# Experts: a new layout of the gates in DRAM, an earlier place for a load in the code, and other buffers for the last residuals

## The chip, the cores and the metric

One core of one Trainium2 chip runs the whole kernel. The metric is device time in microseconds (us); the kernel before took 4202.12 us (median of 3 runs, 4198.15 to 4209.2). A core has five engines that run beside each other: TensorE (PE; its weight loads are PEld), VectorE (DVE), ScalarE (ACT), GpSimd (POOL) and SyncE (SP). SP here only issues DMAs. All DMAs of the core share 16 DMA engines; those that SP issues go through one hardware queue (q1), the indirect gathers that POOL issues through another (q0).

## The reference, cut to what matters

The block is a trunk layer over 1024 tokens of width 1024 (two mixing branches, then a retrieval over experts). The change lies in the retrieval and in the end of the block:

```python
def peer(h, wq, subkeys, u_tab, v_tab):
    ...
        s1, i1 = lax.top_k(s[:, :, 0], PEER_TOPK)
        s2, i2 = lax.top_k(s[:, :, 1], PEER_TOPK)
        ...
        idx = e1 * PEER_KEYS + e2
        gate = jax.nn.softmax(sc, axis=-1).astype(hb.dtype)
        act = jax.nn.gelu(jnp.einsum('td,thkd->thk', hb, u_sel), approximate=False) * gate
        return jnp.einsum('thk,thkd->td', act, v_sel)
...
        h_lat = h_lat + g2_l * peer(f_l, ...)
    return rmsnorm(h_lat, final_norm)
```

Each token picks 128 of 16384 experts (8 heads of 16). An expert is a row of `u_tab` and a row of `v_tab`, 1024 numbers each. The result is multiplied by a gain row `g2_l`, added to the stream `h_lat`, and normalised.

## The kernel before, in words

The 1024 tokens are treated in two ways. Five blocks of 128 tokens (640 tokens, `TD`) are computed densely: the experts form 128 tiles of 128 experts, every tile's scores are computed for all 640 tokens and multiplied by a gate that is zero where a token did not pick the expert. The other three blocks (384 tokens) are computed by gathering: for each of the 128 picks POOL issues one indirect DMA of 128 rows of `u` (or `v`), 768 gathers of 512 KB in all, and DVE multiplies each gathered buffer (`rows`, 7 buffers) into a running sum `e_p`.

**Gates.** In a first stage `spread` makes the dense gates. For each 32 tokens it fills a tile `r_st` of 128 partitions (expert within its tile) by 128 tiles by 32 tokens, and SP writes it to DRAM as one of the 20 slices of `G` (line 1471). A partition's piece is 16 KB in one run, on both sides.

**The expert loop** (`run`) goes over 32 groups of four tiles. For a group, `gates` (line 1614) loads `x_g`: for each of 128 partitions 20 pieces (one per 32 tokens) of four tiles by 32 tokens, which is 512 bytes each. `up` makes the scores of one tile: PE multiplies `x_raw` (loaded by SP, split in a high and a low part on ACT and on DVE or POOL) with the tokens into `x_s` (line 1634), ACT applies the gelu into `x_a`, DVE multiplies with `x_g` (line 1651), ACT and DVE split the product (`x_ah`, `x_al`). For 48 of the tiles (`AHEAD`) the scores were computed during the first stage, written to DRAM as `A`, and `up` loads them instead (line 1647). `down` multiplies the group's products with the `v` rows into PSUM `x_acc` (line 1674), and DVE adds that to the sum `x_o` (line 1680). The `v` rows come in halves of 512 columns: SP loads `x_vr` (2 buffers, 256 KB each, line 1602), ACT and POOL split it into `x_vh` and `x_vl` (lines 1605, 1606). The next load of `x_vr` waits until POOL has made the `x_vl` of the one two before it.

**The end.** `finish` closes a gathered block: it loads the block of `h`, the gain row `g` and the final norm's row `fin` into `rows` buffers, forms g times sum plus h, and `norm` squares it on ACT into the buffer of `h`, scales it on DVE and writes it out. `last_half` does the same for the five dense blocks: it loads the gain and the norm row once more, loads five blocks of `h` into `rows` buffers, lets POOL do the residual of the first 512 columns (lines 1569, 1570) and DVE that of the second half.

**Order.** The code is recorded in program order, and a scheduler with a simulated clock sets the order of instructions on each engine. Each engine and SP's queue then run strictly in that order: an instruction that waits holds up all behind it on its engine.

Of the kernel before, what the change touches and what calls it, by code (L numbers as in the profile page):

```python
# [10 lines left out]
F32 = mybir.dt.float32  # L11
# [10 lines left out]
D = 1024  # L22
# [1182 lines left out]
def colrows(t, n, c0=0, w=D):  # L1205

    return bass.AP(tensor=t.tensor, offset=t.offset + 8 * n * D + c0, ap=[[D, 8], [64 * D, 16], [1, w]])
# [69 lines left out]
ND = 5  # L1277
TD = ND * 128
NG = NB - ND
NT = 128  # L1280
GT = 32
SC = 4
# [8 lines left out]
class Route:  # L1291
# [94 lines left out]
    def second(self, b, wk):  # L1386
# [25 lines left out]
        nc.scalar.activation(pof, pos, AF.Copy)  # L1412
        up = wk.tile([128, 8, 16], F32, name="r_up", bufs=1)
        V.tensor_scalar(up, pof[:, 0], 4.0, None, op0=ALU.is_ge)
        V.scalar_tensor_tensor(pof[:, 2], pof[:, 2], 12.0, pof[:, 0], op0=ALU.subtract, op1=ALU.subtract)
        V.tensor_sub(pof[:, 3], pof[:, 3], pof[:, 1])
# [24 lines left out]
    def spread(self, b, ef, g, wk, ps, pq):  # L1441

        K, nc = self.K, self.K.nc
        V = nc.vector
        p = ps.tile([128, 4, 128], F32, name="qt", bufs=1)
        for j, x in enumerate((ef[:, 1], ef[:, 0], g)):
            nc.tensor.transpose(p[:, j], x, K.ident)
        T = wk.tile([128, 3, 128], F32, name="r_T", bufs=2)
        nc.scalar.activation(T, p[:, :3], AF.Copy)
        for q in range(128 // GT):  # L1450
            st = wk.tile([128, 128, GT], F32, name="r_st", bufs=2)
            for t8 in range(GT // 8):
                t0 = q * GT + t8 * 8
                ts = slice(t0, t0 + 8)
                io = self.iota[:, None, :].to_broadcast([128, 8, 128])
                e0 = wk.tile([128, 8, 128], F32, name="r_e0", bufs=2)
                V.tensor_tensor(e0, io, T[:, 0, ts, None].to_broadcast([128, 8, 128]), op=ALU.is_equal)  # L1457
                e2 = wk.tile([128, 8, 128], F32, name="r_e2", bufs=3)
                V.tensor_tensor(e2, io, T[:, 1, ts, None].to_broadcast([128, 8, 128]), op=ALU.is_equal)  # L1459
                e1 = wk.tile([128, 8, 128], F32, name="r_e1", bufs=2)  # L1460
                nc.gpsimd.tensor_mul(e1[:, :GP], e0[:, :GP], T[:, 2, t0:t0 + GP, None].to_broadcast([128, GP, 128]))
                for m in range(GP, 8):
                    nc.scalar.activation(e1[:, m], e0[:, m], AF.Copy, scale=T[:, 2, t0 + m:t0 + m + 1])
                for t4 in range(2):
                    pg = pq.tile([128, 4, 128], F32, name="qg", bufs=3)
                    for m in range(4):
                        nc.tensor.matmul(pg[:, m], e1[:, t4 * 4 + m], e2[:, t4 * 4 + m], start=True, stop=True)
                    o = t8 * 8 + t4 * 4
                    nc.scalar.activation(st[:, :, o:o + 4], pg.rearrange("p t e -> p e t"), AF.Copy)
                yield  # L1470
            nc.sync.dma_start(K.T["G"][b * (128 // GT) + q], st)


class Experts:
# [77 lines left out]
    def finish(self, b, acc):  # L1552

        V = self.K.nc.vector
        h, g, fin = self.row(), self.row(), self.row()
        self.K.nc.sync.dma_start(h, self.K.T["h1"][b * 128:(b + 1) * 128, :])
        self.ends(g, fin)
        V.tensor_mul(g, g, acc)
        V.tensor_add(g, g, h)
        self.norm(b, g, h, fin)  # L1560

    def ends(self, g, fin):

# [7 lines left out]

    def norm(self, b, acc, h, fin):
        K, nc = self.K, self.K.nc
        ss = self.gp.tile([128, 1], F32, name="f_ss", bufs=2)
        nc.scalar.activation(h, acc, AF.Square, accum_out=ss)
        r = K.rstd(self.gp, ss, D, [128, 1], "f_n")
        nc.vector.scalar_tensor_tensor(acc, acc, r[:], fin, op0=ALU.mult, op1=ALU.mult)
        nc.sync.dma_start(colrows(K.o["out"], b), acc)
# [30 lines left out]
    def gates(self, e):  # L1609

        K, nc, wk = self.K, self.K.nc, self.wk
        n = TD // GT
        t = wk.tile([128, n, SC, GT], F32, name="x_g", bufs=GB)
        nc.sync.dma_start(t, K.T["G"].rearrange("q p e t -> p q e t")[:, :, e:e + SC, :])
        return t

    def score(self):
# [20 lines left out]
    def up(self, g, m):  # L1638

        K, nc, wk = self.K, self.K.nc, self.wk  # L1640
        e = SC * g + m
        if m == 0:
            self.g4 = self.gates(e)
            self.A[g] = []
        if e in AHEAD:
            a = wk.tile([128, TD], F32, name="x_a", bufs=XA)
            nc.sync.dma_start(a, K.T["A"][AHEAD.index(e)])
        else:
            a = self.score()
        av = a.rearrange("p (q t) -> p q t", t=GT)  # L1650
        (nc.gpsimd if self.turn('m', MP) else nc.vector).tensor_mul(av, av, self.g4[:, :, m, :])
        hi = wk.tile([128, TD], F32R, name="x_ah", bufs=AB)
        lo = wk.tile([128, TD], F32R, name="x_al", bufs=AB)
        K.split(a, hi, lo)
        self.A[g].append((hi, lo))

    def ahead_v(self, n):

        while len(self.V) < n and self.nv < 2 * NT:
            g, r = divmod(self.nv, 2 * SC)  # L1660
            half, m = divmod(r, SC)
            self.V[g, half, m] = self.load_v(SC * g + m, half)
            self.nv += 1
# [18 lines left out]
    def last_half(self):  # L1682

        g = NT // SC - 1
        gate, fin = self.row(), self.row()
        self.ends(gate, fin)
        for half in range(2):
            hs = slice(half * 512, (half + 1) * 512)
            for b in range(ND):
                if half == 0:  # L1690
                    if b == 0:
                        self.h = []
                    self.h.append(self.row())
                    self.K.nc.sync.dma_start(self.h[b], self.K.T["h1"][b * 128:(b + 1) * 128, :])
                else:
                    self.down(g, 1, b)
                self.residual(self.K.nc.vector if half else self.K.nc.gpsimd, self.acc[:, b, hs], self.h[b][:, hs], gate[:, hs])
                if half:
                    self.norm(b, self.acc[:, b], self.h[b], fin)

    def pour(self, rb):

# [7 lines left out]
    def run(self, pool, wk, ps):  # L1710
        self.wk, self.ps = wk, ps
        self.acc = pool.tile([128, ND, D], F32, name="x_o")
        left = 256 * NG - int(self.done)
        n = NT // SC

        share = (left - LASTG) / (2 * ND * (n - 1) + ND + 2.6 * (NT - NE))
        self.A, self.V, self.nv = {}, {}, 0
        self.ahead_v(SC)
        for m in range(SC):
            self.up(0, m)  # L1720
            self.some(2.6 * share if m not in AHEAD else 0)
        for g in range(n):
            units = [(h, b) for h in range(2 if g < n - 1 else 1) for b in range(ND)]
            for u, (h, b) in enumerate(units):
                if g < n - 1 and u in UPS:
                    e = SC * (g + 1) + UPS.index(u)
                    self.up(g + 1, UPS.index(u))
                    if e not in AHEAD:
                        self.some(2.6 * share)
                self.down(g, h, b)  # L1730
                self.some(share)
            if g:
                self.A.pop(g - 1, None)
        for _ in self.rows:
            pass
        self.last_half()


# [46 lines left out]
XA = 2  # L1785
# [7 lines left out]
AHEAD = [4 * g + m for g in range(32) for m in range(2 - g % 2)]  # L1793
U_ORDER = AHEAD + [e for e in range(128) if e not in AHEAD]
EF = 1
GB = 2
# [3 lines left out]
def back(K):  # L1800
    T, dr = K.T, K.dram
    T["h1"] = dr.tile([L, D], F32, name="d_h1")
    T["f"] = dr.tile([L, D], F32, name="d_f")
    T["G"] = dr.tile([TD // GT, 128, 128, GT], F32, name="d_G")
    T["A"] = dr.tile([max(NE, 1), 128, TD], F32, name="d_A")
    with K.pool("keep") as keep, K.pool("xg") as gp, K.pool("ft", right=True) as ft, K.pool("xu", right=True) as xu:
        R = Route(K, keep)
        R.fTd = [ft.tile([128, 8, TD], F32R, name="fT" + n) for n in "hl"]
        X = Experts(K, R, gp, xu)
        with ExitStack() as late:  # L1810
            with K.pool("rm", right=True) as mid:
                R.tables(mid)
                out_proj(K, R)
                X.gps = late.enter_context(K.pool("xgp", space=PSUM))
                peer(K, X, R)
            X.pour(RB2)
# [107 lines left out]
```

## Time and profile before

| | |
|---|---|
| median of 3 runs | 4202.12 us |
| profiled execution, its own time | 4209.43 us |
| its span in the trace | 4207.5 us |
| PE busy | 3807.4 us (90%) |
| DVE busy | 3385.1 us (80%) |
| POOL busy | 2045.4 us (49%) |
| granted clock of PE, mean | 0.954 |

The durations come from one execution of 4209.43 us, which is 7.3 us above the median. Its span lies 1.9 us below its own time. The expert loop begins at about 2560 us of the span and ends at about 4166 us, with the last matmul.

### The profile page before, as it was taken

How to read it: one execution, taken by the hardware profiler on the slowest of the kernel's cores; microseconds unless marked ns; L12 is line 12 of the kernel's file. 1: busy time of each engine (PE TensorE's matmuls, PEld its weight loads, DVE VectorE, ACT ScalarE, POOL GpSimd, SP SyncE). 2: the span in 40 equal slices, each digit the busy share in tenths (PEclk: the TensorE clock that was granted, in tenths of full speed). 3: DMA queues.
4: the chain of work that ended last, by engine and by line, in shares of the span. 5: the costliest groups of instructions: out<-in, count | busy, mean ns of one | idle time of the engine just before them, and what ended most of it. 6: DMA issues, size and time to landing. Idle time of an engine off the chain costs nothing.

```text
span 4207.5 us, 60407 instructions
## 1 busy us (share of the span) xinstructions
PE 3807.4 (90%) x21993; PEld 3346.8 (80%) x21993; DVE 3385.1 (80%) x5997; ACT 1389.8 (33%) x2674; POOL 2045.4 (49%) x1643
## 2 busy tenths in 40 slices
PE   5999999898898997789999968899989999999996
PEld 3787887787888896689999867788878888788785
DVE  5665787546799795599999996788878889888798
ACT  3233333325563121242236664222222222222221
POOL 2232323344343121066435445666667776777675
PEclk8999999998899998899999999999999999999998
DMA  6333333466766446567546547899989999999897
GB/s 204 110 124 98 125 120 127 133 204 206 235 210 204 152 145 177 175 236 267 197 158 231 191 161 259 284 321 318 348 300 337 326 327 346 337 322 338 317 330 259
DMA packets 509673, 974.12 MB, mean 232 GB/s; under 512 B 33771, under 2 KB 291231, under 8 KB 506432
## 3 DMA queue, kind: packets, MB, share of 16 engines
q1 hardware_dynamic: 395616, 557.25, 40.4%
q0 software_dynamic: 110880, 405.98, 26.3%
q10 hardware_dynamic: 2880, 7.03, 0.5%
q8 instruction: 173, 2.83, 0.3%
q14 instruction: 124, 1.02, 0.1%
HBM read 823.20 MB, written 146.95 MB: 231 GB/s over the span
## 4 chain that ended last, share of the span: by engine, by line
PE 39%; DVE 22%; DMA 13%; issue 7%; POOL 6%; ACT 3%; SPq 1%; POOLq 0%; DVEq 0%; ACTq 0%
PE x_acc L1674 9%; PE x_s L1634 8%; PE mm L199 7%; DMA x_vr<-in_peer_v_dram 6%; POOL rows L1511 3%; DVE rows L1535 3%; PE pe L1134 2%; PE hy L850 2%; POOL x_vl L1606 2%; DVE r_e L1459 2%; PE tp L850 1%; DVE r_e L1457 1%; PE hx L850 1%; DMA s_e<-d_cum 1%; DMA rows<-in_peer_u_dram,ids 1%
## 5 line engine op out<-in xcount | busy, mean ns | idle before, releaser
L1634 PE MATMUL x_s<-fTh,x_uh 128*128 128x320 f32 x2048 | 642.9, 314 | 15.0 <-ACT x_a L1635 15.0
L1634 PE MATMUL x_s<-fTh,x_ul 128*128 128x320 f32 x2048 | 640.1, 313 | 5.5 <-DVE x_ul L1595 5.5
L1634 PE MATMUL x_s<-fTl,x_uh 128*128 128x320 f32 x2048 | 640.5, 313 | 0.0
L1674 PE MATMUL x_acc<-x_vl,x_ah 128*128 128x512 f32 x1280 | 517.2, 405 | 18.3 <-POOL x_vl L1606 18.3
L1674 PE MATMUL x_acc<-x_vh,x_ah 128*128 128x512 f32 x1280 | 451.9, 405 | 85.0 <-ACT x_vh L1605 61.4
L1548 DVE SCALAR_TENSOR_TENSOR e_p<-rows,e_a,e_p 128x1024 f32<-128x1024 f32 x381 | 489.6, 1285 | 35.1 <-DMA rows<-in_peer_v_dram,ids 27.6
L1674 PE MATMUL x_acc<-x_vh,x_al 128*128 128x512 f32 x1280 | 512.2, 402 | 0.0
L1511 POOL DMA_INDIRECT rows<-in_peer_u_dram,ids x384 | 417.7, 1088 | 177.7 <-DVE rows L1535 54.5
L1535 DVE SCALAR_TENSOR_TENSOR rows<-rows,e_p 128x1024 f32<-128x1024 f32 x384 | 456.2, 1210 | 34.1 <-DMA rows<-in_peer_u_dram,ids 33.7
L1511 POOL DMA_INDIRECT rows<-in_peer_v_dram,ids x384 | 402.8, 1049 | 133.1 <-issue 62.9
L1606 POOL TENSOR_TENSOR x_vl<-x_vr,x_vh 128x512 fp32r<-128x512 f32 x256 | 340.1, 1332 | 191.0 <-ACT x_vh L1605 187.6
L1634 PEld LDWEIGHTS x_s<-fTh,x_uh 128*128 128x128 f32 x2048 | 390.5, 191 | 30.1 <-ACT x_a L1635 19.9
L1634 PEld LDWEIGHTS x_s<-fTh,x_ul 128*128 128x128 f32 x2048 | 389.7, 190 | 15.5 <-DVE x_ul L1595 6.9
L1634 PEld LDWEIGHTS x_s<-fTl,x_uh 128*128 128x128 f32 x2048 | 390.4, 191 | 9.4
L1674 PEld LDWEIGHTS x_acc<-x_vh,x_ah 128*128 128x128 f32 x1280 | 242.1, 194 | 139.3 <-ACT x_vh L1605 69.3
L1674 PEld LDWEIGHTS x_acc<-x_vl,x_ah 128*128 128x128 f32 x1280 | 249.8, 195 | 72.0 <-POOL x_vl L1606 26.2
L1605 ACT ACTIVATE x_vh<-x_vr 128x512 fp32r<-128x512 f32 x256 | 160.0, 627 | 423.3 <-DMA x_vr<-in_peer_v_dram 349.6
L1674 PEld LDWEIGHTS x_acc<-x_vh,x_al 128*128 128x128 f32 x1280 | 249.0, 195 | 49.4
L1595 POOL TENSOR_TENSOR x_ul<-x_raw,x_uh 128x1024 fp32r<-128x1024 f32 x57 | 140.3, 2461 | 281.6 <-ACT x_uh L1594 281.3
L199 PE MATMUL mm<-xh,whi 128*128 128x512 f32 (+1 forms) x784 | 263.9, 412 | 7.4 <-DVE acc L235 3.6
L199 PE MATMUL mm<-xl,whi 128*128 128x512 f32 (+1 forms) x784 | 263.8, 411 | 7.1 <-DVE xl L51 7.1
L1594 ACT ACTIVATE x_uh<-x_raw 128x1024 fp32r<-128x1024 f32 x128 | 135.2, 1057 | 400.1 <-PE x_s L1634 355.4
(382 smaller groups left out, 8704.3 us busy)
## 6 DMA issues: line engine op xcount, KB each, us to landing
x_raw<-in_peer_uT_dram SPq DMA_DIRECT2D x128, 512.0 KB
x_vr<-in_peer_v_dram SPq DMA_DIRECT2D x256, 256.0 KB
d_G<-r_st SPq DMA_DIRECT2D x20, 2048.0 KB
x_g<-d_G SPq DMA_DIRECT2D x32, 1280.0 KB
wraw<-in_w_mod_dram SPq DMA_DIRECT2D x32, 1024.0 KB
wraw<-in_w_in_dram SPq DMA_DIRECT2D x24, 1024.0 KB
wk_w<-d_WK SPq DMA_DIRECT2D x24, 1024.0 KB
d_kr<-h_k SPq DMA_DIRECT2D x32, 512.0 KB
```

What stands on the lines that cost most here:

```text
L199: nc.tensor.matmul(p, w[:, k], x[j][:, k, t0:t0 + n], start=(k == 0 and q == 0), stop=(k == 7 and q == 2))
L850: nc.tensor.matmul(out, self.m[mats][:, tl, :], x, start=(n == 0), stop=(n == len(terms) - 1))
L1134: nc.tensor.matmul(p, a[:, k], w[:, ss], start=(k == 0 and q == 0), stop=(k == n - 1 and q == 2))
L1511: nc.gpsimd.indirect_dma_start(out=r, out_offset=None, in_=table, in_offset=bass.IndirectOffsetOnAxis(ap=ids[:, j:j + 1], axis=0))
L1535: nc.vector.scalar_tensor_tensor(r, r, 1.0, f, op0=ALU.mult, op1=ALU.mult, accum_out=d[:, j:j + 1])
L1548: nc.vector.scalar_tensor_tensor(acc, r, a[:, j:j + 1], acc, op0=ALU.mult, op1=ALU.add)
L1594: nc.scalar.activation(hi, raw, AF.Copy)
L1595: self.pace = (nc.vector if self.turn('u', UR if self.n < NE else UP) else nc.gpsimd).tensor_sub(lo, raw, hi.bitcast(F32)).ins
L1605: nc.scalar.activation(hi, raw, AF.Copy)
L1606: self.pace = nc.gpsimd.tensor_sub(lo, raw, hi.bitcast(F32)).ins
L1634: nc.tensor.matmul(s[:, :SW], w[:, k], x[:, k, ms], start=(k == 0 and q == 0), stop=(k == 7 and q == 2))
L1674: self.K.nc.tensor.matmul(p, a[x][:, bs], v[w], start=(m == 0 and q == 0), stop=(m == SC - 1 and q == 2))
```

## The change

There are three parts. (a) `G` in DRAM gets the order group, partition, 32-token slice, tile and token. The write of a slice then puts 32 pieces of 512 bytes per partition in 32 places, and a group's load reads one run of 10240 bytes per partition. (b) The load of an `AHEAD` tile stands in the code at the end of the step before. (c) At the end, the blocks of `h` of the dense part go to the two `x_g` buffers (two blocks in each, and one in a `rows` buffer), the last `finish`'s gain and norm rows are kept and used by `last_half`, and `finish` works in the PSUM sum: it multiplies the sum in place, adds it to `h`, and squares into the sum.

```diff
-            nc.sync.dma_start(K.T["G"][b * (128 // GT) + q], st)
+            nc.sync.dma_start(K.T["G"][:, :, b * (128 // GT) + q].rearrange("g p e t -> p g e t"),
+                              st.rearrange("p (g e) t -> p g e t", e=SC))
...
-        V.tensor_mul(g, g, acc)
-        V.tensor_add(g, g, h)
-        self.norm(b, g, h, fin)
+        V.tensor_mul(acc, acc, g)
+        V.tensor_add(h, h, acc)
+        self.norm(b, h, acc, fin)
+        self.gains = g, fin
...
-        nc.sync.dma_start(t, K.T["G"].rearrange("q p e t -> p q e t")[:, :, e:e + SC, :])
+        nc.sync.dma_start(t, K.T["G"][e // SC])
...
         if e in AHEAD:
-            a = wk.tile([128, TD], F32, name="x_a", bufs=XA)
-            nc.sync.dma_start(a, K.T["A"][AHEAD.index(e)])
+            a = self.pre.pop(e) if e in self.pre else self.load_a(e)
...
+        if e + 1 in AHEAD:
+            self.pre[e + 1] = self.load_a(e + 1)
...
-        gate, fin = self.row(), self.row()
-        self.ends(gate, fin)
...
+        gate, fin = self.gains
+        halves = [slice(half * 512, (half + 1) * 512) for half in range(2)]
+        for b in range(ND):
+            self.residual(self.K.nc.gpsimd, self.acc[:, b, halves[0]], self.h[b][:, halves[0]], gate[:, halves[0]])
+        for b in range(ND):
+            self.down(g, 1, b)
+            self.residual(self.K.nc.vector, self.acc[:, b, halves[1]], self.h[b][:, halves[1]], gate[:, halves[1]])
+            self.norm(b, self.acc[:, b], self.h[b], fin)
+
+    def load_h(self):
+
+        self.h = []
+        for b in range(ND):
+            if b == ND - 1:
+                h = self.row()
+            elif b % 2:
+                h = t[:, D:2 * D]
+            else:
+                t = self.wk.tile([128, TD // GT, SC, GT], F32, name="x_g", bufs=GB).rearrange("p q e t -> p (q e t)")
+                h = t[:, :D]
+            self.K.nc.sync.dma_start(h, self.K.T["h1"][b * 128:(b + 1) * 128, :])
+            self.h.append(h)
...
-    T["G"] = dr.tile([TD // GT, 128, 128, GT], F32, name="d_G")
+    T["G"] = dr.tile([NT // SC, 128, TD // GT, SC, GT], F32, name="d_G")
```

On SP's queue in the expert loop, here some groups after its start, the kernel before has these rows (`x_raw` the tiles of `u`, `x_vr` the halves of `v`, `x_a<-d_A` the scores made ahead, `x_g` the gates):

```order
L1602 DMA x_vr<-in_peer_v_dram 128x512 x2
L1647 DMA x_a<-d_A 128x640
L1602 DMA x_vr<-in_peer_v_dram 128x512 x2
L1584 DMA x_raw<-in_peer_uT_dram 128x1024
L1614 DMA x_g<-d_G 128x20x128
L1647 DMA x_a<-d_A 128x640
```

At the same place the changed kernel has:

```order
L1604 DMA x_vr<-in_peer_v_dram 128x512 x2
L1662 DMA x_a<-d_A 128x640
L1604 DMA x_vr<-in_peer_v_dram 128x512 x2
L1586 DMA x_raw<-in_peer_uT_dram 128x1024
L1616 DMA x_g<-d_G 128x2560
L1662 DMA x_a<-d_A 128x640
```

Nothing moved here: the loads of `x_a` stand where they stood, and only the shape of the load of `x_g` differs.

At the end of SP's queue the kernel before has, behind the last loads of `v` (`d_h` is the stream, `d_rows` the gain row):

```order
L1647 DMA x_a<-d_A 128x640
L1602 DMA x_vr<-in_peer_v_dram 128x512 x19
L1556 DMA rows<-d_h_13947 128x1024
L1565 DMA rows<-d_rows 128x1024
L1566 DMA rows<-in_final_norm_dram 128x1024
L1565 DMA rows<-d_rows 128x1024
L1566 DMA rows<-in_final_norm_dram 128x1024
L1694 DMA rows<-d_h_13947 128x1024 x4
L1578 DMA out_dram<-rows 8x16x1024
L1694 DMA rows<-d_h_13947 128x1024
L1578 DMA out_dram<-x_o 8x16x1024 x5
```

And the changed kernel:

```order
L1662 DMA x_a<-d_A 128x640
L1604 DMA x_vr<-in_peer_v_dram 128x512 x3
L1713 DMA x_g<-d_h_13947 128x1024 x2
L1604 DMA x_vr<-in_peer_v_dram 128x512 x10
L1713 DMA x_g<-d_h_13947 128x1024 x2
L1604 DMA x_vr<-in_peer_v_dram 128x512 x5
L1557 DMA rows<-d_h_13947 128x1024
L1567 DMA rows<-d_rows 128x1024
L1604 DMA x_vr<-in_peer_v_dram 128x512
L1568 DMA rows<-in_final_norm_dram 128x1024
L1713 DMA rows<-d_h_13947 128x1024
L1580 DMA out_dram<-rows 8x16x1024
```

Four of the five loads of `h` moved ahead among the loads of `v`, two loads went, and the last load of `v` now stands behind the `h` and the gain row of the last `finish`.

On POOL the kernel before ends with (gathers, low parts of `v`, then the residuals of the first halves):

```order
L1511 DMA rows<-in_peer_v_dram,ids_13967 128x1024 x3
L1606 TENSOR_TENSOR x_vl<-x_vr,x_vh 128x512
L1511 DMA rows<-in_peer_v_dram,ids_13967 128x1024
L1606 TENSOR_TENSOR x_vl<-x_vr,x_vh 128x512 x2
L1569 TENSOR_TENSOR x_o<-x_o,rows 128x512 x5
L1570 TENSOR_TENSOR x_o<-x_o,rows 128x512 x5
```

And the changed kernel with:

```order
L1512 DMA rows<-in_peer_v_dram,ids_13967 128x1024 x3
L1608 TENSOR_TENSOR x_vl<-x_vr,x_vh 128x512
L1512 DMA rows<-in_peer_v_dram,ids_13967 128x1024
L1608 TENSOR_TENSOR x_vl<-x_vr,x_vh 128x512 x2
L1571 TENSOR_TENSOR x_o<-x_o,rows 128x512 x5
L1572 TENSOR_TENSOR x_o<-x_o,x_g 128x512
L1608 TENSOR_TENSOR x_vl<-x_vr,x_vh 128x512
L1572 TENSOR_TENSOR x_o<-x_o,x_g 128x512 x3
```

The last low part of `v` now stands behind the five products with the gain row and one sum.

## Rows read from the trace of the kernel before

**Rows 1.** The page: busy time by engine, and the slices of the span (40 of them, digits in tenths).

```profile
PE 3807.4 (90%) x21993; PEld 3346.8 (80%) x21993; DVE 3385.1 (80%) x5997; ACT 1389.8 (33%) x2674; POOL 2045.4 (49%) x1643
...
PEclk8999999998899998899999999999999999999998
DMA  6333333466766446567546547899989999999897
```

**Rows 2.** Busy time by stage (window, its length, then busy us and instructions of PE, PEld, DVE, ACT, POOL, then the granted clock, the DMA share and the DMA rate): the making of the gates, the expert loop, the end.

```profile
2200.00:2560.00 360.00, 300.14 (x2205) 287.34 (x2204) 350.07 (x496) 241.90 (x611) 166.35 (x108) 0.97 0.53 197
...
2600.00:4120.00 1520.00, 1424.90 (x7304) 1247.35 (x7303) 1288.61 (x1503) 376.83 (x608) 1061.56 (x905) 0.97 0.92 325
4120.00:4207.50 87.50, 45.98 (x203) 37.36 (x201) 68.78 (x69) 16.66 (x31) 47.44 (x39) 0.78 0.70 249
```

**Rows 3.** Waits of PE in the expert loop, 2600 to 4120 us (who waited for what: us in total, times, longest).

```profile
PE x_acc L1674 <- ACT x_vh L1605: 59.5, 21, 7.2
PE x_acc L1674 <- POOL x_vl L1606: 17.5, 16, 2.9
PE x_acc L1674 <- DVE x_o L1680: 11.9, 6, 3.3
PE x_s L1634 <- ACT x_a L1635: 5.8, 5, 2.3
```

**Rows 4.** The chain that ended last, in order of time (start us, length us, what): the longest pieces early in the loop, and the first ones of it.

```profile
2558.07 7.24 DMA d_G<-r_st
...
2666.41 4.07 DMA x_vr<-in_peer_v_dram
2675.82 19.13 DMA x_vr<-in_peer_v_dram
2740.98 19.14 DMA x_vr<-in_peer_v_dram
```

**Rows 5.** The timeline of SP's queue around two of these pieces (start us, us that the issue took, line, DMA).

```profile
2674.53 0.42 SPq L1614 DMA_DIRECT2D x_g<-d_G  x1
...
2738.13 0.38 SPq L1614 DMA_DIRECT2D x_g<-d_G  x1
2740.98 11.67 SPq L1602 DMA_DIRECT2D x_vr<-in_peer_v_dram  x1
```

**Rows 6.** Two short stretches behind such pieces (columns as in Rows 2).

```profile
2691.23:2701.47 10.24, 5.73 (x14) 4.47 (x15) 3.86 (x3) 2.10 (x4) 4.65 (x5) 0.50 0.59 191
2759.50:2766.30 6.80, 5.42 (x15) 4.64 (x16) 3.49 (x1) 2.53 (x4) 5.22 (x4) 0.50 0.41 131
```

**Rows 7.** DMA queues from 2594.0 to 2600.4 us, where one load of `x_g` runs with few gathers beside it (packets, MB, share of the 16 engines' time).

```profile
q1 hardware_dynamic: 2632, 1.46, 80.8%
```

**Rows 8.** The same from 2742.1 to 2758.8 us, where one load of `x_g` runs beside many gathers.

```profile
q0 software_dynamic: 1133, 4.11, 63.9%
q1 hardware_dynamic: 2959, 2.13, 41.5%
```

**Rows 9.** The same from 2899.1 to 2903.9 us, a load of `x_raw` (128 pieces of 4 KB) beside gathers (pieces of 4 KB).

```profile
q0 software_dynamic: 282, 1.02, 58.3%
q1 hardware_dynamic: 141, 0.52, 31.9%
```

**Rows 10.** The same from 2548.4 to 2553.5 us, a write of `d_G` alone (pieces of 16 KB).

```profile
q1 hardware_dynamic: 115, 1.88, 87.7%
```

**Rows 11.** The same from 1131.4 to 1135.2 us, a write of `d_z` and loads beside it, all in small pieces (512 bytes and less).

```profile
q1 hardware_dynamic: 1469, 0.74, 72.0%
```

**Rows 12.** Waits in the loop of DVE for the scores made ahead.

```profile
DVE x_a L1651 <- DMA x_a<-d_A: 29.5, 9, 7.8
```

**Rows 13.** The timeline of the end, SP, POOL, DVE and ACT apart (start us, us, engine, line, operation, and in brackets the idle time before it and what ended it).

```profile
4157.41 0.32 SPq L1565 DMA_DIRECT2D rows<-d_rows  x1
...
4160.90 1.29 POOL L1606 TENSOR_TENSOR x_vl<-x_vr,x_vh 128x512 fp32r<-128x512 f32 x1 [4.51 <-ACT x_vh L1605]
4165.84 7.54 POOL L1569 TENSOR_TENSOR x_o<-x_o,rows 128x512 f32<-128x512 f32 x5 [3.65 <-DMA rows<-d_rows]
4191.43 1.70 POOL L1570 TENSOR_TENSOR x_o<-x_o,rows 128x512 f32<-128x512 f32 x1 [6.45 <-DMA rows<-d_h]
...
4173.85 0.68 DVE L1680 TENSOR_TENSOR x_o<-x_o,x_acc 128x512 f32<-128x512 f32 x1
4174.45 1.69 DVE L1559 TENSOR_TENSOR rows<-rows 128x1024 f32<-128x1024 f32 x1
4195.97 0.16 DVE L59 RECIPROCAL f_n_r<-f_n_s 128x1 f32<-128x1 f32 x1
4196.24 1.28 DVE L1577 SCALAR_TENSOR_TENSOR x_o<-x_o,f_n_r,rows 128x1024 f32<-128x1024 f32 x1
...
4176.17 1.06 ACT L1575 ACTIVATE rows<-rows 128x1024 f32<-128x1024 f32 x1 [15.35 <-DVE rows L1559]
4177.34 1.28 ACT L58 ACT_TABLE_LOAD   x1
4178.63 0.29 ACT L58 ACTIVATE f_n_s<-f_ss,eps 128x1 f32<-128x1 f32 x1
```

**Rows 14.** The chain that ended last, at the end (as in Rows 4).

```profile
4162.25 3.69 PE x_acc L1674 x8
...
4181.16 10.13 DMA rows<-d_h
```

More of the change, by code (lines that the diff above doesn't have):

```diff
@@ L1573, in norm @@
         K, nc = self.K, self.K.nc
-        ss = self.gp.tile([128, 1], F32, name="f_ss", bufs=2)
+        ss = self.gp.tile([128, 1], F32, name="f_ss", bufs=4)
         nc.scalar.activation(h, acc, AF.Square, accum_out=ss)
@@ L1655, in up, with load_a @@
         self.A[g].append((hi, lo))
+        if e + 1 in AHEAD:
+            self.pre[e + 1] = self.load_a(e + 1)
+    def load_a(self, e):
+        a = self.wk.tile([128, TD], F32, name="x_a", bufs=XA)
+        self.K.nc.sync.dma_start(a, self.K.T["A"][AHEAD.index(e)])
+        return a
     def ahead_v(self, n):
@@ L1684, in last_half @@
         g = NT // SC - 1
-        gate, fin = self.row(), self.row()
-        self.ends(gate, fin)
[L1687 to L1699, printed above, removed]
+        gate, fin = self.gains
[18 more added lines that the diff above has]
+            self.h.append(h)
     def pour(self, rb):
@@ L1716, in run @@
         share = (left - LASTG) / (2 * ND * (n - 1) + ND + 2.6 * (NT - NE))
-        self.A, self.V, self.nv = {}, {}, 0
+        self.A, self.V, self.nv, self.pre = {}, {}, 0, {}
         self.ahead_v(SC)
@@ L1735, in run @@
             pass
+        self.load_h()
         self.last_half()
```

## The prediction, made before the changed kernel ran

> **What bounds the kernel now.** I read the page first, then the busy times by stage, then PE's waits, then the chain, and last the DMA queues in short windows. The page says that PE is busy for 90% of the span and that the DMA engines are nearly full in the last two fifths [rows 1]. All that the change touches lies there, in the making of the gates before it, and in the end. The stages [rows 2] show three different limits. While the gates are made DVE has the work: 350 of 360 us, with the DMA engines at 0.53. In the expert loop PE is busy for 1425 of 1520 us, DVE for 1289, and the DMA engines are at 0.92. At the end PE is busy for only 46 of 87.5 us: there it is a chain.
>
> So the loop can win what PE loses. PE waits there for 95 us, 59.5 of them in 21 waits that ACT's high part of `v` ends, the longest 7.2 us [rows 3]. ACT has little work, so the question is what ACT waited for. The chain answers: a load of `x_vr` takes 4.1 us in one place and 19.1 us in two others [rows 4]. SP's queue shows what stands right ahead of these two: each time a load of `x_g`, the gates, 1.3 and 2.9 us before [rows 5]. Both go through q1. SP even needs 11.7 us to issue the load behind the second, instead of some 0.3 [rows 5, 13]: the queue is full.
>
> These waits cost twice. Behind them the granted clock stands at 0.50 for a while, 1.2 GHz instead of 2.4, as in the two stretches of [rows 6]. Over the loop the clock is 0.97 [rows 2], which is 0.03 x 1520 = 46 us lost. All that PE can lose in the loop is thus some 95 + 46 = 141 us.
>
> **The gates in larger pieces.** A load of `x_g` has 128 x 20 = 2560 pieces of 512 bytes. With few gathers beside it, a packet of q1 takes 0.808 x 6.4 us x 16 / 2632 = 31 ns [rows 7], so the load needs 2560 x 31 / 16 = 5.0 us of all engines, and 6.4 us in the clock. Beside many gathers it took 16.7 us [rows 8]. Afterwards it has 128 pieces of 10 KB. No load with such pieces is in the trace. The nearest row is the write with 16 KB pieces: 0.877 x 5.1 x 16 / 115 = 622 ns [rows 10], so 389 ns for 10 KB and 8 x 389 = 3.1 us for the load. That is the lower end. Beside gathers the queues take turns. With 4 KB pieces on both, q0 gets two for one of q1 (282 to 141), each of 0.583 x 4.8 x 16 / 282 = 159 ns [rows 9]. If a 10 KB piece is one turn, the load takes 8 x (389 + 318) = 5.7 us. If it is cut into turns of 4 KB, it has 20 turns of 159 + 318 ns, 9.5 us. That is the upper end. I take 5.7 us, since the 16 KB pieces went whole. Against 16.7 us the `x_vr` behind it comes 7 to 11 us sooner, and 3 us sooner where gathers are few.
>
> The longest of PE's waits for it is 7.2 us, so nearly all of the 59.5 us could go. I take three quarters, 45 us: with DVE at 0.85 and the DMA engines above 0.9 something else will be late next, probably the low part of `v` on POOL (17.5 us already) or DVE's sums (11.9 us) [rows 3]. Of the 46 us of clock I take 18, since these waits are 63% of the waiting time but only 21 of 48 waits. The loop gives 63 us, with 20 and 110 as ends.
>
> The Trainium skill speaks against this. Its page "DMA: Bandwidth & Descriptors", section "Specifications", gives 512 bytes as the smallest piece at line rate; below that a write becomes a read and a write. By it the load would be as fast now as later, and the loop would give nothing. The trace does not agree: 512 bytes in 31 ns is 264 GB/s over 16 engines [rows 7], and 4 KB in 159 ns is 412 GB/s [rows 9].
>
> The price is paid where the gates are written: 32 pieces of 512 bytes for each of 16 KB. Small pieces went in 0.72 x 3.8 x 16 / 1469 = 30 ns, writes and loads together [rows 11], so 32 x 30 = 954 ns instead of 622 ns, and a write of 8 such per engine takes 7.6 us instead of 5.0. Nineteen of the twenty lie beside DVE's 350 of 360 us; the DMA share there goes from 0.53 to some 0.67. The last one is on the chain [rows 4], since the first `x_g` waits for it: +2.7 us, of which that `x_g` gives back 1.9. I count +1. Were the cover gone, all twenty would cost 53 us.
>
> **The load one step sooner.** It does nothing. The order of SP's queue is the same before and after: the scheduler had already moved these loads forward, and the two buffers of `x_a` are taken in the same order. DVE's 29.5 us of waits for them [rows 12] stay, apart from what a shorter `x_g` ahead of them gives. I count 0.
>
> **`finish` in PSUM.** The sum's buffer is free for the next block only after the addition and ACT's squaring. Before, it was free after the product. The dots of the next gathered block start later by the addition, the squaring, a table load and a small activation: 1.7 + 1.1 + 1.3 + 0.3, some 4 us [rows 13]. That happens twice in the loop. DVE stands in that wait, with the evictions of PSUM behind it, and PE has four PSUM buffers before it notices. Between 0 and 8 us; I take +3.
>
> **The end.** Before, the residuals wait for `h` in `rows` buffers, with a piece of 10.1 us on the chain [rows 14] and 6.5 us of idle POOL [rows 13]. That goes. What is late next is the last `x_vl`: POOL now has five products and one sum ahead of it, 7.5 + 1.7 = 9.2 us, and they wait for the gain row. Before, that row was issued at 4157.41 and freed POOL at 4165.84 [rows 13]. The row now used comes one `finish` earlier, and I put its landing at 4162. Then the last `x_vl` is ready at about 4173 instead of 4162.2, and the last matmul ends near 4177 instead of 4165.9 [rows 14]. DVE then has for each of five blocks an eviction, a product, a sum, and the scaling, 3 x 0.68 + 1.28 and a reciprocal of 0.16, 3.5 us. It begins at 4173 and ends at about 4191, against 4197.5 [rows 13]. That is 6.5 us less. The loads of `h` now pass between the last loads of `v`, 1 MB at a time, and the second pair waits for the last product with the gates; I take 2.5 us off. The end gives 4 us, between 10 (the wait goes, nothing takes its place) and -9 (the 9.2 us in full, nothing gained).
>
> **Sum.** -63 + 1 + 0 + 3 - 4 = -63 us. The profiled execution took 4209.4 us, so 4146; it was 7.3 us above the median, so 4139 us.
>
> **Rivals.**
> - *All of it goes.* The `x_vr` is never late again, and with PE never idle the clock stays up: 59.5 + 46 in the loop and 10 at the end, 115 us, which gives 4087. For it: the longest wait is shorter than what the load gains. Against it: three of the engines stand at 0.85 or more.
> - *Most is given back.* The loop gives 20 us, because the gathers or POOL's low part are late instead: 4182. For it: the DMA engines are at 0.92, and fewer waits of PE mean the same bytes in less time. Against it: the bytes now need less DMA time, 29 x 1.9 = 55 us less.
> - *Small pieces cost nothing.* By a full rate at 512 bytes the loop gives 0: 4209.4 + 1 + 3 - 4 - 7.3 = 4202. The trace [rows 7, 8] speaks against it.
> - *The gathers starve, and it gets slower.* Eight pieces of 389 ns per engine hold the gathers back for 3.1 us per group. DVE takes the gathered rows in order, so it stands, and the evictions behind it make PE stand: 29 groups x 3.1 = 90 us, less the 63 gained, 27 us more: 4229. It decides only where DVE has no spare time, and DVE has (1520 - 1289) / 29 = 8 us per group [rows 2].
>
> **Chances.** About 0.3%, 12.6 us, is what a measurement of this kernel can tell from no change. My forecast has 0.55 (4110 to 4165); all of it 0.18; given back 0.15, a fifth of that within 0.3%; small pieces free 0.05; starving 0.07. Faster: 0.55 + 0.18 + 0.12 = 0.85; same: 0.03 + 0.05 = 0.08; slower 0.07. The range reaches into the case where all goes, and up to where the given-back case ends: 4082 to 4190.
>
> **What would show it.** The loads of `x_vr` behind an `x_g` take 6 to 10 us, and SP issues them in under 1 us. PE's waits for ACT's high part in the loop fall from 59.5 us to some 15, and the loop's clock rises to 0.98 or more. DVE's waits for gathers grow by a few us. The making of the gates keeps its length, with a DMA share near 0.67. At the end, POOL's five products stand ahead of the last `x_vl`, and the last matmul is later against the last gather than before. I am wrong if a load of `x_g` still takes over 10 us, or if PE's waits move to DVE's evictions with the same sum.

## The result, and the profile after

The changed kernel takes 4132.01 us (median of 4 runs, 4128.36 to 4138.53). The kernel before took 4205.66 us beside it, so the ratio is 0.9828, with an interval of 0.9807 to 0.9849: about 74 us less, 1.7%. The prediction said 4139 us. The profiled execution took 4128.4 us; that is 81 us less than the execution shown before. Some 7 of these are the choice of executions: the one before lies 3.8 us above its median, the one after 3.6 below.

The page of the changed kernel, as in [rows 1]:

```profile
PE 3781.7 (92%) x21993; PEld 3322.5 (81%) x21993; DVE 3394.6 (82%) x5997; ACT 1391.5 (34%) x2674; POOL 2038.8 (49%) x1643
...
PEclk9999999999799999789999998999999999999998
DMA  6333333366776445747727756799999899999997
```

Its busy times by stage, as in [rows 2]: making of the gates, the loop, the end. The loop's window ends at the last gathers, as that of before does.

```profile
2200.00:2560.00 360.00, 302.44 (x2207) 289.65 (x2206) 350.86 (x496) 242.13 (x611) 166.01 (x108) 0.97 0.63 196
...
2600.00:4044.00 1444.00, 1397.09 (x7324) 1226.40 (x7323) 1302.40 (x1507) 378.49 (x609) 1062.84 (x904) 0.99 0.93 343
4044.00:4126.30 82.30, 46.66 (x187) 35.16 (x185) 61.10 (x66) 16.46 (x30) 45.40 (x40) 0.83 0.65 242
```

The gain is in the loop. Its window is 76 us shorter, 1444 us instead of 1520; the end gives the rest of the 81 us, some 5.6. PE stands for 1444 - 1397 = 47 us, where it stood for 95, so 48 us less. The other 28 us are less busy time, although there are 20 more matmuls in the window: a matmul takes 1397.09 / 7324 = 190.8 ns on average, where it took 1424.9 / 7304 = 195.1. That is 4.3 ns less, or 32 us for 7300 matmuls, and it goes with the clock, 0.99 for 0.97. The DMA engines move the same bytes at 343 GB/s instead of 325, and are as full as before. The making of the gates keeps its length, with the DMA share at 0.63 for 0.53.

PE's waits in the loop, as in [rows 3]:

```profile
PE x_acc L1682 <- POOL x_vl L1608: 18.2, 12, 3.8
PE x_acc L1682 <- DVE x_o L1688: 15.5, 12, 2.5
PE x_acc L1682 <- ACT x_vh L1607: 8.3, 6, 1.9
PE x_s L1636 <- ACT x_a L1637: 4.4, 5, 1.2
```

The waits for ACT's high part fell from 59.5 us to 8.3, and the longest wait of all from 7.2 us to 3.8. The others stayed, within 4 us. The chain of the loop shows the same from the loads' side (start us, length us, what; the three longest loads of `x_vr` on it, 2600 to 4044 us):

```profile
2635.51 11.37 DMA x_vr<-in_peer_v_dram
...
3097.33 7.28 DMA x_vr<-in_peer_v_dram
...
3863.55 9.42 DMA x_vr<-in_peer_v_dram
```

None of them is near the 19 us of [rows 4], but the first lies above the 6 to 10 us that I had forecast. SP's queue around the first of the three, as in [rows 5]:

```profile
2634.10 0.33 SPq L1616 DMA_DIRECT2D x_g<-d_G  x1
2635.51 1.64 SPq L1604 DMA_DIRECT2D x_vr<-in_peer_v_dram  x2
```

The load still stands right behind an `x_g`, but two of them are issued in 1.64 us, where the same two took 9.16 in the kernel before. In 22 places of the loop a load of `v` is issued right behind an `x_g`. Its issue takes 0.33 us there on average, where it took 5.95 (longest 11.67). From the issue of the `x_g` to the last piece of that load of `v` it is 10.6 us on average (longest 12.5), where it was 14.4 (longest 19.4), with the pieces counted in the order of issue. The queues beside another load of `x_g`, from 2897.7 to 2904.2 us, as in [rows 8]:

```profile
q1 hardware_dynamic: 249, 1.59, 60.9%
q0 software_dynamic: 267, 1.00, 39.4%
```

The load passes within 6.5 us beside some 260 gathered pieces. By the DMA records of the trace, its first to last piece lie 5.8 us apart on average (4.3 to 8.2 in single loads); before it was 11.4 (6.2 to 18.5). The pieces went whole, 10240 bytes in a median of 385 ns.

DVE's waits in the loop (2600 to 4040 us) for gathers, and for the scores made ahead [rows 12]:

```profile
DVE rows L1536 <- DMA rows<-in_peer_u_dram,ids: 30.4, 32, 2.9
DVE e_p L1549 <- DMA rows<-in_peer_v_dram,ids: 30.1, 33, 4.1
...
DVE x_a L1652 <- DMA x_a<-d_A: 3.9, 3, 2.8
```

The gathers cost DVE 60.5 us, where they cost 31.7 + 26.0 (2600 to 4100 us); they don't starve. The waits for `x_a` fell from 29.5 us to 3.9, though these loads stand where they stood.

The end, as in [rows 13]: POOL, then DVE.

```profile
4086.42 6.19 POOL L1571 TENSOR_TENSOR x_o<-x_o,rows 128x512 f32<-128x512 f32 x5 [1.79 <-DMA rows<-d_rows]
4092.57 1.26 POOL L1572 TENSOR_TENSOR x_o<-x_o,x_g 128x512 f32<-128x512 f32 x1
4093.79 2.24 POOL L1608 TENSOR_TENSOR x_vl<-x_vr,x_vh 128x512 fp32r<-128x512 f32 x1
4095.99 4.19 POOL L1572 TENSOR_TENSOR x_o<-x_o,x_g 128x512 f32<-128x512 f32 x3
...
4097.34 0.69 DVE L1688 TENSOR_TENSOR x_o<-x_o,x_acc 128x512 f32<-128x512 f32 x1 [2.43 <-PE x_acc L1682]
...
4099.57 1.17 DVE L1572 TENSOR_TENSOR x_o<-x_o,x_g 128x512 f32<-128x512 f32 x1
4100.66 0.67 DVE L1688 TENSOR_TENSOR x_o<-x_o,x_acc 128x512 f32<-128x512 f32 x1
```

The wait for `h` is gone, and the last `x_vl` stands behind POOL's five products and a sum. The chain that ended last, as in [rows 14]:

```profile
4080.91 5.45 DMA rows<-d_rows
...
4096.08 1.24 PE x_acc L1682 x2
```

The load of 10.1 us has left the chain, and a load of the gain row of 5.45 us has come in. From the last gather to the end of the span it is 48.3 us (issued at 4078.0), where it was 53.9 (4153.6).

### The profile page after: what moved, and what is told of

Read it like the earlier page. It is cut to its first block, busy times and chain, and to the rows that moved or that the text cites. A ratio compares the mean times of both kernels' runs of the same rounds, so it can differ in the third digit from the quotient of the medians.

```text
span 4126.3 us, 60371 instructions
## 1 busy us (share of the span) xinstructions
PE 3781.7 (92%) x21993; PEld 3322.5 (81%) x21993; DVE 3394.6 (82%) x5997; ACT 1391.5 (34%) x2674; POOL 2038.8 (49%) x1643
## 4 chain that ended last, share of the span: by engine, by line
PE 44%; DVE 22%; DMA 9%; issue 7%; POOL 5%; ACT 3%; SPq 0%; POOLq 0%; DVEq 0%; ACTq 0%
PE x_acc L1682 12%; PE x_s L1636 10%; PE mm L199 7%; DVE rows L1536 3%; PE pe L1134 2%; PE hy L850 2%; POOL rows L1512 2%; DMA s_e<-d_cum 2%; DMA x_vr<-in_peer_v_dram 2%; DVE r_e L1459 2%; PE tp L850 2%; DVE r_e L1457 2%; DMA rows<-in_peer_v_dram,ids 1%; PE hx L850 1%; DVE e_p L1549 1%
## 5 line engine op out<-in xcount | busy, mean ns | idle before, releaser
L1512 POOL DMA_INDIRECT rows<-in_peer_u_dram,ids x384 | 417.4, 1087 | 177.7 <-DVE rows L1536 48.3
L1682 PE MATMUL x_acc<-x_vh,x_ah 128*128 128x512 f32 x1280 | 442.4, 397 | 38.3 <-DVE x_o L1688 16.8
```

What stands on the lines that cost most here:

```text
L1512: nc.gpsimd.indirect_dma_start(out=r, out_offset=None, in_=table, in_offset=bass.IndirectOffsetOnAxis(ap=ids[:, j:j + 1], axis=0))
L1682: self.K.nc.tensor.matmul(p, a[x][:, bs], v[w], start=(m == 0 and q == 0), stop=(m == SC - 1 and q == 2))
```

## The experiments

My theory was: the time went with the queue. What `v` waits for is how long an `x_g` stands ahead of it in SP's queue, and that is set by the size of the gates' pieces; the other parts are worth nothing. The rivals were that another part of the change gives the gain, and that pieces of 512 bytes are not slow in themselves. Ratios are against the kernel before on the same chip.

**The layout alone.** The three edits of `G`, made to the kernel before:

```diff
-        nc.sync.dma_start(t, K.T["G"].rearrange("q p e t -> p q e t")[:, :, e:e + SC, :])
+        nc.sync.dma_start(t, K.T["G"][e // SC])
```

> Only the new layout of the gates; the code of the loads made ahead, of finish and of the end as before. The order of every engine and of SP's queue is the same as before the change, so only the sizes of the DMA pieces differ. My theory: the layout is the whole gain of the loop, so this kernel takes 4137 us (4130 to 4146), with PE's wait for ACT's high part of v at 5 to 15 us as in the changed kernel, and the end as long as before (about 54 us from the last gather's issue). Rival: the shorter end and the earlier load share the gain, then this takes 4150 to 4170 us.

It took 4126.3 us (4123.27 to 4134.52), ratio 0.9826 [0.9799, 0.9854]. PE's waits in its loop:

```profile
PE x_acc L1675 <- POOL x_vl L1607: 17.8, 10, 3.9
PE x_acc L1675 <- DVE x_o L1681: 12.8, 9, 2.5
PE x_acc L1675 <- ACT x_vh L1606: 6.0, 4, 2.0
```

The layout is the whole gain, and the profile of its loop is that of the full change. The time lies 4 us below the range that I had given; the ratio is that of the full change. The waits for `x_a` went here too (2.3 us), without the second part of the change.

**All but the layout.** The changed kernel with the three edits of `G` undone:

```diff
-        nc.sync.dma_start(t, K.T["G"][e // SC])
+        nc.sync.dma_start(t, K.T["G"].rearrange("q p e t -> p q e t")[:, :, e:e + SC, :])
```

> The changed kernel with the old layout of the gates (written in 16 KB pieces, read in 512-byte pieces); the rest of the change stays, and so does the order of every engine. My theory: the loop is as slow as before the change, with some 60 us of PE waiting for ACT's high part of v, and only the end is some 5 us shorter: 4199 us (4190 to 4206). Rival, the load one step sooner or the end gave half: 4165 us.

It took 4204.58 us (4192.07 to 4208.31, 10 runs), ratio 1.0002 [0.9985, 1.002]. Its first wait:

```profile
PE x_acc L1681 <- ACT x_vh L1606: 55.4, 22, 7.0
```

So the earlier place of the load, `finish` in PSUM and the new end are together worth nothing that can be measured; by the interval, a sum of up to some 8 us either way would not show. The earlier place alone was not run.

**512 bytes from a run of 10240.** The new layout in DRAM, but the tile in SBUF has a gap of 16 bytes behind every 512, so a partition has 20 pieces on that side:

```diff
-        t = wk.tile([128, n, SC, GT], F32, name="x_g", bufs=GB)
-        nc.sync.dma_start(t, K.T["G"][e // SC])
+        t = wk.tile([128, n // KQ, KQ * SC * GT + KPAD], F32, name="x_g", bufs=GB)
+        v = t[:, :, :KQ * SC * GT]
+        nc.sync.dma_start(v, K.T["G"][e // SC].rearrange("p (c k) e t -> p c (k e t)", k=KQ))
...
+KQ = 1
+KPAD = 4
```

> The changed kernel, with the gates in DRAM in the new order, one run of 10 KB per partition, but read in 2560 pieces of 512 bytes: the buffer in SBUF has a gap of 16 bytes behind every 512 bytes. The order of all engines is that of the changed kernel. My theory, the number of pieces decides: as slow as the kernel with the old layout, 4199 us (4190 to 4206), and a load of the gates takes 6 to 18 us. Rival, the scattered reads in DRAM were the cost: as fast as the changed kernel, 4132 us, a load 4 to 8 us.

It took 4151.96 us (4143.98 to 4154.35), ratio 0.9875 [0.9843, 0.9907], so my expectation failed. The first line is its DMA traffic from 2600 to 4020 us, the second, from the view of waits, PE's wait for ACT:

```profile
DMA packets 145340, 480.46 MB, mean 338 GB/s; under 512 B 16016, under 2 KB 16016, under 8 KB 140484
```

```profile
PE x_acc L1683 <- ACT x_vh L1607: 13.3, 8, 4.2
```

There are no packets of 512 bytes: both "under 512 B" and "under 2 KB" count 16016, so nothing lies between. The records show 160 packets of 8192 bytes for each load, so small pieces that are neighbours in DRAM went together, 16 to a packet. A load took 6.9 us on average. The run couldn't tell what it was meant to tell, but it gave a middle point: loads of 11.4, 6.9 and 5.8 us go with 4205, 4152 and 4132 us. The issue of the load of `v` behind an `x_g` is still slow, 4.7 us on average instead of 5.95, though the packets are few. DVE's product with `x_g` keeps its 0.82 us (median) beside the gaps.

**2 KB and 5 KB.** The same edit with larger pieces; in the records those of 2048 bytes stay apart.

```diff
+KQ = 4
+KPAD = 4
```

> As the run with 512-byte pieces, but with a gap behind every 2 KB: 640 pieces per load of the gates, 40 per engine. Two theories part here. By turns (beside gathers q1 gets one piece for two gathered pieces of 4 KB) a load takes some 40 x (84 + 318) ns = 16 us beside many gathers, as long as with 512-byte pieces, and the kernel takes 4180 us (4165 to 4200). By the engines' time alone (84 ns for 2 KB is nearly the full rate) the load needs 3.4 us of all engines against 3.1, and the kernel is as fast as the changed one, 4135 us.

It took 4145.31 us (4139.56 to 4149.69), ratio 0.9861 [0.983, 0.9893], with this wait:

```profile
PE x_acc L1683 <- ACT x_vh L1607: 16.8, 11, 3.3
```

That is far from what one piece per turn of the queues would give (4180), and above the 4135 of the engines' time alone. Counted in the order of issue, a load's 640 pieces lie some 6.6 us apart (3 to 10), and not 16. The issue behind an `x_g` is down to 0.36 us here. With 5 KB (`KQ = 10`):

> As the run with pieces of 2 KB, but with a gap behind every 5 KB: 256 pieces per load of the gates. Theory as it stands now: what counts is how long the load stands in SP's queue ahead of the next load of v, and that shrinks with larger pieces; between the run with 2 KB (4145 us) and the changed kernel (4132 us): 4137 us (4130 to 4143). Rival, every gap in SBUF costs the same: 4145 us or more, as with 2 KB.

4134.1 us (4133.36 to 4140.91), ratio 0.9834 [0.9813, 0.9856]: not to be told apart from the whole run.

The time from the issue of an `x_g` to the last piece of the load of `v` right behind it puts all these runs in one order: 14.4 us before, 12.3 with 512 bytes side by side, 11.8 with 2 KB, 11.0 with 5 KB and 10.6 with the change go with 4205, 4152, 4145, 4134 and 4132 us. How much of it is SP's blocked issue and how much the passage of the pieces was not parted.

**The gates on ACT's queue.** In the kernel before, the load of `x_g` is issued by ACT, so that it no longer stands ahead of `v` in SP's queue; then the same in the kernel with the layout alone. Both have the same order on all engines, which in the loop is not that of the kernels above.

```diff
-        nc.sync.dma_start(t, K.T["G"].rearrange("q p e t -> p q e t")[:, :, e:e + SC, :])
+        nc.scalar.dma_start(t, K.T["G"].rearrange("q p e t -> p q e t")[:, :, e:e + SC, :])
```

> The kernel before the change, old layout, but the gates are loaded through ACT's queue and not SP's, so that no load of v stands behind them in one queue. The scheduler orders the loop anew, so this run is read against the next one, which has the same order on every engine and only the new layout. My theory, the loads of v wait behind the gates in the same queue: PE's waits for ACT's high part of v fall below 25 us and this kernel is within 20 us of the next. Rival, the 5 us of all 16 DMA engines that the small pieces take are the cost: this one is 60 to 75 us slower than the next.

> The layout alone, with the gates loaded through ACT's queue; the same order on every engine as the run before it. My theory: about as fast as the layout alone with SP's queue, 4120 to 4140 us, and at most 20 us faster than the run before it. Rival: 60 to 75 us faster than the run before it.

With pieces of 512 bytes it took 4150.12 us (4142.19 to 4155.93), ratio 0.9869 [0.9854, 0.9884]; with 10 KB 4155.32 us (4151.74 to 4158.03), 0.9884 [0.9869, 0.99]. The waits of PE and ACT with 512 bytes:

```profile
PE x_acc L1674 <- ACT x_vh L1605: 15.2, 8, 2.6
...
ACT x_vh L1605 <- DMA x_vr<-in_peer_v_dram: 206.3, 75, 9.2
```

ACT's wait in the kernel before, over the same 2600 to 4040 us:

```profile
ACT x_vh L1605 <- DMA x_vr<-in_peer_v_dram: 301.0, 90, 15.3
```

PE's wait with 10 KB:

```profile
PE x_acc L1675 <- ACT x_vh L1606: 12.9, 11, 1.5
```

In SP's queue the size of the pieces is worth 74 us, and out of it, in this order, nothing. It is so although a load of small pieces took even longer there, 16.5 us on average, than one of 10 KB, 5.6. So it is the place ahead of `v` in one queue that made small pieces dear, not the DMA time they use. The move alone, with 512 bytes, gives 53 us, its new order included. Both are slower than the layout alone, and the 4120 to 4140 us that I had expected with 10 KB failed. I put that down to their other order; that wasn't tried apart. ACT's work of issuing the loads is another candidate: before `x_vh` the view of waits has 19 to 20 us of idle ACT for which it names no releaser, where the layout alone has 0.3.

**The end in other orders.** First POOL's residuals behind the last `x_vl`:

```diff
-            self.residual(self.K.nc.gpsimd, self.acc[:, b, halves[0]], self.h[b][:, halves[0]], gate[:, halves[0]])
+            with self.K.tc.issue_after(self.pace):
+                self.residual(self.K.nc.gpsimd, self.acc[:, b, halves[0]], self.h[b][:, halves[0]], gate[:, halves[0]])
```

> The changed kernel with POOL's products of the last residual put behind the last low part of v; the order of PE and of SP's queue stays, on DVE and ACT only the order of the last rows differs. My theory: at the end PE waits 6.9 us for that low part, which stands behind 7.5 us of products and a sum, so the last matmul comes 5 us sooner and the kernel takes 4128 us, 4 less than the changed one. Rival, DVE or the products themselves set the end: no difference, 4132 us.

4126.49 us (4121.95 to 4135.69), ratio 0.9825 [0.9812, 0.9839]: not to be told from the change. POOL and DVE at its end:

```profile
4080.58 1.29 POOL L1608 TENSOR_TENSOR x_vl<-x_vr,x_vh 128x512 fp32r<-128x512 f32 x1 [2.91 <-ACT x_vh L1607]
4081.83 7.26 POOL L1571 TENSOR_TENSOR x_o<-x_o,rows 128x512 f32<-128x512 f32 x5
...
4090.09 1.74 DVE L1572 TENSOR_TENSOR x_o<-x_o,x_g 128x512 f32<-128x512 f32 x1
4091.76 3.42 DVE L1571 TENSOR_TENSOR x_o<-x_o,rows 128x512 f32<-128x512 f32 x2
4095.11 1.74 DVE L1572 TENSOR_TENSOR x_o<-x_o,x_g 128x512 f32<-128x512 f32 x1
```

At 4126 us the run doesn't part the 4128 of my theory from the rival's 4132. The last `x_vl` comes 10.2 us after the last gather's issue (4070.4) instead of 15.8, and yet it is 49.5 us from there to the end. DVE's own work is next: beside POOL's residuals its products and sums take 1.74 us instead of 0.68.

Then the loads of `h` behind the last rows that `finish` loads:

```diff
-            self.K.nc.sync.dma_start(h, self.K.T["h1"][b * 128:(b + 1) * 128, :])
+            with self.K.tc.issue_after(self.lastrow):
+                self.K.nc.sync.dma_start(h, self.K.T["h1"][b * 128:(b + 1) * 128, :])
```

> The changed kernel with the five loads of h at the end issued behind the last finish's loads, so that none stands between the last loads of v; with that the scheduler also puts POOL's products behind the last low part of v. My theory: the two megabytes between the loads of v cost the last group 7 us (the last gather came at 4078.0 us against 4071.1 us in the kernel with the layout alone), and the shorter end is worth some 4 to 8 us when nothing is in its way: 4118 us (4112 to 4124), faster than the changed kernel and than the layout alone (4126 us). Rival, the end is bound by the loads of h wherever they stand: 4126 to 4132 us.

4133.05 us (4129.7 to 4135.98), ratio 0.9833 [0.9817, 0.9846]: a miss, it is as the change. The last gather came at 4082.6 us, not at 4071. The run before has it at 4070.4 with the loads of `h` where the change has them, so the 7 us that I had put down to them lie within what differs from run to run. The 2.5 us that I had charged for these loads can't be seen; but here the order of DVE, ACT and POOL near the end differs too.

**No loads of gates.** They are loaded for the first two groups alone, and these two tiles are used throughout:

```diff
+        if e // SC < GB:
+            t = wk.tile([128, n, SC, GT], F32, name="x_g", bufs=GB)
+            nc.sync.dma_start(t, K.T["G"][e // SC])
+            self.gt = getattr(self, "gt", []) + [t]
+        return self.gt[e // SC % GB]
```

> The changed kernel, but the gates are loaded for the first two groups alone and used for all others, so the output is not the reference's; the scheduler orders the loop somewhat anew. It shows what the loads of the gates still cost. Theory, v's wait in the queue behind the gates is nearly gone already (8 us of PE's waits, some more of the clock): 4115 us (4100 to 4130). Rival, the loop is bound by the 16 DMA engines, which save 30 loads of 3 us: 4040 to 4070 us.

4085.86 us (4080.36 to 4093.38), ratio 0.9719 [0.9695, 0.9744], some 46 us below the change and between what the two theories gave, so both missed. PE's waits in its loop, 2600 to 4000 us, and then the busy times there (columns as in [rows 2]):

```profile
PE x_acc L1684 <- DVE x_o L1690: 6.7, 7, 3.0
PE x_acc L1684 <- POOL x_vl L1608: 3.7, 6, 1.2
PE x_s L1638 <- ACT x_a L1639: 2.6, 2, 1.4
PE x_acc L1684 <- ACT x_vh L1607: 0.7, 1, 0.7
```

```profile
2600.00:4000.00 1400.00, 1386.07 (x7339) 1225.58 (x7339) 1315.03 (x1512) 379.19 (x610) 1066.81 (x907) 1.00 0.91 327
```

All of PE's waits fell, from 46 us to 14, and the clock is at 1.00. So in this run also the waits that the view puts down to POOL and to DVE went with the loads of the gates, and the change left some 46 us, where it took 74. How much of that is the place in the queue, how much the 39 MB themselves, and how much the somewhat different order of this loop, isn't told apart.

## Why the prediction was right, and where its sizes were off

- **What bounds it.** Right: the gain came from PE's waits for `x_vr` behind `x_g` and from the clock behind these waits; the other parts gave nothing that can be measured. The layout alone shows that it is the layout, and the loads on another queue that it is the place ahead of `v`.
- **The load of `x_g`.** 5.7 us taken, 5.8 measured; 389 ns for a piece taken, 385 measured. The `x_vr` behind it comes some 4 us sooner on average; the longest fell by 7, the lower end of the 7 to 11 that I had read off one slow load. And the 5.7 was luck in part: the reason was right by its size only. I had let the queues take turns of one piece of q1 for two gathered ones. By that, pieces of 2 KB had to be slow, and they weren't. The Trainium skill has the likely reason ("DMA: Bandwidth & Descriptors", "Queues, rings and completion order"): an engine goes round the queues by packets of several descriptors each. The run with 2 KB agrees that a turn holds more than one small piece; how many, no run here shows.
- **The waits.** 45 us taken, and 48 measured for all waits of PE, and 51 for those behind ACT's high part. "Something else will be late next" was right in kind, but hardly cost anything: POOL and DVE rose by 4 us together.
- **The clock: the mis-sized term.** 18 us taken, 32 measured. I shared the 46 us out by the number of waits (21 of 48 would go), and 35 are left. But the loss did not go by their number: the stretches at half clock cost 12 us of the loop, where they had cost 51 (granted clock, summed over all stretches). The other runs bear that out (2600 to 4040 us): 33 waits with a loss of 31 us with 512 bytes on ACT's queue, 53 waits with 19 us with 10 KB there. Nor does it go by the longest wait alone: with pieces of 2 KB that is 3.8 us, as in the change, and the loss is 27 us. The old layout in the changed kernel lost 39 us (2600 to 4120 us) with about the same waits as the kernel before. What it goes by stays open. With that term at 32 the sum is -77, against the -81 of the two profiled executions.
- **The price of the writes.** +1 taken; the first `x_g` was issued at 2566.4 us, where it was 2565.4. The other runs have it between 2560.8 and 2566.6 in SP's queue, with either layout, so 1 us can't be read from it. The share of 0.67 came to 0.63, and DVE's time covered it.
- **The load one step sooner.** 0 taken, and all but the layout gives 1.0002. Its waits fell by 26 us all the same, by the shorter queue (28.5 us in all but the layout, 2.3 in the layout alone); that was named, but not counted.
- **`finish` in PSUM.** The hand-over of the sum to the next block takes 5.2 us instead of 1.3 in this trace, the 4 us forecast (product at 2944.7, the next block's sum begun at 2949.9). Whether it costs the +3 us isn't to be seen beside the rest.
- **The end.** Every step came: POOL's products ahead of the last `x_vl`, the last matmul 10.5 us later against the last gather (25.6 us behind it, before 15.1; forecast 11), DVE's end 6.5 us sooner (37.4 us behind it, before 43.9; forecast 6.5). The last matmul before ended at 4168.7 us, not at the 4165.9 that I had read off the chain. The 2.5 us for the loads of `h` found no support. The profile gives 5.6 us in all, the times by themselves nothing.
- **The rivals.** *Small pieces cost nothing* fell. The Trainium skill's line on 512 bytes in "DMA: Bandwidth & Descriptors", "Specifications" does not hold for this load: 31 ns for 512 bytes [rows 7] is 264 GB/s, and 10240 bytes in 385 ns are 426. *The gathers starve* fell too: DVE's waits for them rose by 3 us, not 90. *All of it goes* fell: 46 us of PE's waits stayed. It named 4087 us, which is where the kernel came out without the gates' loads (4086), not with larger ones. *Most is given back* needed a new wait that isn't there.

## What to carry to other kernels

When a matmul waits for a load, look at what stands ahead of that load in its own DMA queue: what is waited for is how long that neighbour holds up the issue and the queue. Larger pieces took that away here (74 us), and another queue did most of it (53 us, with another order). Scattered writes are cheap in a stage where an engine covers them; the same pieces on the reading side stood in the way of the bottleneck. A wait of the tensor engine can cost twice: here 48 us of waits went, and another 32 us with the clock. That second price was not proportional to the number of waits, so it is better read from the granted clock of several runs than shared out by their count.

## What the hardware showed that I had not expected

- Pieces of 512 bytes with gaps on the SBUF side, but side by side in DRAM, went as packets of 8192 bytes, 160 to a load; pieces of 2 KB, laid in the same way, stayed apart. Such a packet of 8192 bytes took 398 ns (median), more than one whole piece of 10240 (385).
- DVE's sums of two SBUF tiles beside POOL's residuals took 1.17 us, up to 1.74 in the other order, and 0.68 without; its sums with one side in PSUM stayed at 0.67 to 0.69. The Trainium skill ("GPSIMD Engine Reference", "1. Specifications") says that POOL shares its interfaces to SBUF with DVE's instructions of two SBUF inputs; the rows agree.
- The loads of `x_a` came in time, 29.5 us of waits to 3.9, without having moved.
- SP's issue of a load of `v` behind an `x_g` took 5.95 us on average with 2560 pieces in DRAM, 4.7 with 2560 pieces that went as 160 packets, and 0.33 to 0.36 with 640 pieces or fewer.
